# A decoder layer on one core: three activation chunks split straight from PSUM, and x given a second time with its columns on partitions

## The chip, the core and the metric

The kernel runs on one core of a Trainium2 chip. The metric is the device time of one execution in microseconds (us). Five engines matter here, each with its own queue that it works through in order: TensorE (PE in the profile, its weight loads PEld), VectorE (DVE), ScalarE (ACT), GpSimd (POOL) and SyncE (SP). SP issues most of the loads; POOL and ACT issue the others. An engine that waits holds up everything behind it in its own queue.

## The reference, cut to what matters

One layer over 256 rows and 2048 columns, all in float32:

```
h      = rmsnorm(x, g_mix)                       # x * rsqrt(mean(x*x over the row)) * g_mix
proj   = h @ w_in                                # q, k, v of 16 heads, and three gates
o      = stick-breaking / block-sparse / dilated attention, 4 + 6 + 6 heads
merged = sum over the branches of sigmoid(gate) * (o_branch @ w_branch)
x      = x + merged @ w_out
h2     = rmsnorm(x, g_ffn)
gu     = h2 @ w_gu                               # 2 * 5632 columns
x      = x + (silu(gu[:, :5632]) * gu[:, 5632:]) @ w_down
```

q and k of the last 12 heads are normed by row and scaled with `q_gain` and `k_gain`.

## The kernel before

**Products.** A product takes its left factor with the contracted columns on partitions. Each float32 factor is split into a high part, which ScalarE rounds (`copy`, shown as CAST), and a low part, which VectorE subtracts (`tensor_sub`, shown as TENSOR_TENSOR); `split` (lines 104 to 107) issues both. `product` (lines 164 to 169) is then three TensorE instructions: high by high (L167), low weights by high (L168), high weights by low (L169), each 128x128 against 128x512. Weights come in tiles of 128x1024, two steps k of the contraction. The split weights have five rooms each (`w_hi`, `w_lo`), the raw ones four (`w_raw`), and the raw quarters of a pair six (`g_raw`).

**Units.** The first half is a list of units: unit 1 is the v columns of head group 0, unit 2 the first gate, unit 3 the q and k columns of group 0 as a pair. `project` does a single block of columns; `project_pair` does two blocks at once with seven instead of eight products of quarters for the chunks in `WC`, the rest plainly. `begin_pair` already loads and splits the next unit's first quarters. Side work hangs in two lists of generators, `stages` and `slow_stages`; `advance` takes one step of one of them per weight tile. A scheduler orders the instructions of each engine, save where `keep_in_program_order` or `manual_schedule` fixes them.

**The start.** x is loaded in 128x512 pieces (`xc`, `xs`), rows on partitions. TensorE transposes each by four 128x128 instructions against `ident` (`first_columns`, `transpose4`), VectorE multiplies what comes out in PSUM with `g1` (`next_columns`, `to_h`), and the result is split into `h`. `g1` is `g_mix` transposed by TensorE, and `g2` and the q and k gains come the same way from `par`. A few dummy products (`idle`) fill TensorE while the first loads are under way. The rows are squared in unit 1 on ScalarE (`squares`), and their mean gives `rstd`, which `keep_v` multiplies onto the finished v. While the rows are not yet known, v stands in its two PSUM banks (`ps`).

**The gate and up projections.** Eleven units, c = 0 to 10, each a `project_pair` over `w_gu`, then SiLU and product into two tiles `sg`. `to_a` transposes them (four TensorE instructions for each 128 rows, into the PSUM tile `tr`, which has two banks), copies them out (ScalarE, L938), and POOL stores them to `a_mem` in DRAM (L939). The factor of the down projection is read back from there: `take_a` loads a chunk into `a_raw` (POOL, L959) and splits it by L105 into `a_hi` and `a_lo`. For the first three chunks (`ORDER[:EARLY]`, chunks 0, 1 and 2, L968) this is written behind the eleven units, and the scheduler puts it into units 1, 2 and 3 (each carries the chunk of the unit before it) as soon as the data exist; the other eight are taken around the beginning of the down projection.

Of the kernel before, what the change touches and what calls it, by code (L numbers as in the profile page):

```python
# [17 lines left out]
P = 128  # L18
# [33 lines left out]


@with_exitstack
def hybrid_block(ctx: ExitStack, tc: tile.TileContext, x, g_mix, w_in, q_gain, k_gain, w_branch, w_out,
                 g_ffn, w_gu, w_down, rel_bias, onehot, extra, out):
    nc = tc.nc
    x, out = x[0], out[0]

# [10 lines left out]
    nc.scalar.dma_start(gmix, g_mix[0].rearrange("(k p) -> k p", p=P))  # L70

    ident = consts.tile([P, P], F32, name="ident")
    nc.gpsimd.memset(ident, 0.0)
# [26 lines left out]
    def fetch(dst, src):  # L100

        tc.keep_in_program_order(nc.sync.dma_start(dst, src))
# [284 lines left out]
            tc.keep_in_program_order(nc.tensor.matmul(nothing, zeros[:, :P], zeros, start=True, stop=True))  # L387


    NPAR = KT + 2 * H_SOFT  # L390
    par = consts.tile([NPAR, P], F32, name="par")
    tc.keep_in_program_order(nc.gpsimd.dma_start(par[0:KT, :], g_ffn[0].rearrange("(k p) -> k p", p=P)))
    tc.keep_in_program_order(nc.gpsimd.dma_start(par[KT:KT + H_SOFT, :], q_gain[0]))
    tc.keep_in_program_order(nc.gpsimd.dma_start(par[KT + H_SOFT:NPAR, :], k_gain[0]))

    x1 = dram.tile([NT, P, D], F32, name="x1")

    p1 = pool(ph1, "p1", "left")
# [9 lines left out]
    def load_x(c, queue):  # L408
        xc = [half_kb() for _ in range(NT)]
        for t in range(NT):  # L410
            queue(xc[t], x[t * P:(t + 1) * P, c * NB:(c + 1) * NB])
        return xc
# [16 lines left out]
            if pin:  # L429
                tc.keep_in_program_order(sq)  # L430

    ss1 = small.tile([P, NT, 4], F32, name="ss1", bufs=1)
    rstd = small.tile([P, NT], F32, name="rstd", bufs=1)
    g1 = consts.tile([P, KT], F32, name="g1")
    g2 = consts.tile([P, KT], F32, name="g2")
    gq = consts.tile([P, H_SOFT], F32, name="gq")


    V0 = 2 * NH * HD
    xc = [half_kb() for _ in range(NT)]  # L440
    xs = [xc]
# [15 lines left out]
    xs.append(load_x(1, fetch))  # L457
# [5 lines left out]
    xs += [load_x(c, fetch) for c in (2, 3)]  # L463


    columns = {c: [o_raw[:, 4 * i + 2 * t:4 * i + 2 * t + 2, :].rearrange("p h (a q) -> p (h a) q", a=2)
                   for t in range(NT)] for i, c in enumerate(WC)}

    def next_columns(c, t, pt):
        tmp = columns[c][t]  # L470
        nc.vector.tensor_mul(tmp, pt, g1[:, 4 * c:4 * c + 4, None].to_broadcast([P, 4, P]))
        h.put(c, t, tmp)

    held = []

    def first_columns(t, n, w, goes_on=None):

        if not goes_on:
            held.append(tr.tile([P, 4, P], F32, name="tr"))
            for i in range(w):  # L480
                nc.tensor.transpose(held[-1][:, i, :], xc[t][:, (n + i) * P:(n + i + 1) * P], ident)
            if goes_on is not None:
                return
        pt = held[-1]
        k = slice(n, n + w)
        c = columns[0][t][:, k]
        nc.vector.tensor_mul(c, pt[:, 0:w], g1[:, k, None].to_broadcast([P, w, P]))
        nc.scalar.copy(h.hi[:, k, t * P:(t + 1) * P], c)

    def low_part(t):  # L490
# [22 lines left out]
        nc.tensor.matmul(ps0[t], h.plain(t, k)[1], woven(W_HI[k]), start=False, **how)  # L513

    with tc.manual_schedule(engines={mybir.EngineType.PE, mybir.EngineType.DVE, mybir.EngineType.Activation}):
        high(0)
        first_columns(0, 0, 2)
        first_columns(0, 2, 2)
        idle(3)
        high_high(0, 0)  # L520
        first_columns(1, 0, 4, False)
        low(0)
        high(1)
        high_high(0, 1)
        low_part(0)
        high_low(0, 0)
        low_high(0, 0)
        first_columns(1, 0, 4, True)
        low(1)
        low_high(0, 1)  # L530
        high_low(0, 1)
        turned = [transpose4(xs[1][0])]
        high_high(1, 0)
        high_high(1, 1)
        high_low(1, 0)
        high(2)
        low_part(1)
        high_low(1, 1)
        low_high(1, 0)
        low_high(1, 1)  # L540
        low(2)
        high_high(0, 2)
        low_high(0, 2)
        turned.append(transpose4(xs[1][1]))
        high_high(1, 2)
        low_high(1, 2)
        high(3)
        low(3)
        next_columns(1, 0, turned[0])
# [6 lines left out]
        next_columns(1, 1, turned[1])  # L556
        high_low(0, 3)
        high_low(1, 3)


    def rest_of_x():
        for c in range(2, 4):
            for t in range(NT):
                to_h(h, xs[c][t], c, t, g1, c == 3)
                yield
            squares(xs[c - 2], ss1, c - 2, True)
            yield
        squares(xs[2], ss1, 2)
        squares(xs[3], ss1, 3)
# [26 lines left out]
    vec = dram.tile([H_SOFT, NDIST], F32, name="vec")  # L596

    def parameters():
        pp = tr.tile([P, 4 * P], F32, name="tr")
        nc.tensor.transpose(pp[:, :NPAR], par, ident[:NPAR, :NPAR])  # L600
        parT = consts.tile([P, NPAR], F32, name="parT")
        nc.vector.tensor_copy(parT, pp[:, :NPAR])
        nc.vector.tensor_copy(g2, parT[:, 0:KT])
        nc.vector.tensor_mul(gq, parT[:, KT:KT + H_SOFT], parT[:, KT + H_SOFT:NPAR])
# [9 lines left out]
        nc.tensor.matmul(pb[:H_SOFT, :NDIST], rb_sb[:N_BUCKETS, :H_SOFT], oh_sb[:N_BUCKETS, :NDIST], start=True, stop=True)  # L614
# [161 lines left out]
    heads = {}  # L776

    def keep_v(g, ps):
        finish_stages(slow_stages)
# [49 lines left out]
    for (kind, what), after in zip(units, units[1:] + [(None, None)]):  # L829
# [14 lines left out]
                         *((ps0, 4, there) if (kind, what) == ("v", 0) else ()))  # L844
            ahead = begin_pair(*nxt) if nxt else None
        finish_stages(stages)
        if kind == "v":
            keep_v(what, ps)
            if what == 0:
                slow_stages.append(sums_of_h())  # L850
# [80 lines left out]

    a_mem = dram.tile([NF // 4, P, 4, S], F32, name="a_mem")

    def to_a(c, srcs):
        for t in range(NT):
            pt = transpose4(srcs[t])
            st = half_kb().rearrange("p (k q) -> p k q", k=4)
            nc.scalar.copy(st, pt)  # L938
            nc.gpsimd.dma_start(a_mem[c, :, :, t * P:(t + 1) * P], st)  # L939
            yield  # L940
# [175 lines left out]
```

## Time and profile before

| | |
|---|---|
| median of 3 runs | 1387.82 us (1387.64 to 1389.24) |
| the profiled execution's own time | 1387.56 us |
| its span, first to last instruction | 1385.8 us |
| mean granted TensorE clock | 0.994 of full speed |
| PE busy | 1362.3 us, 98% of the span |
| DVE, ACT, POOL busy | 83%, 64%, 8% |

A row of the timeline gives start, duration, engine, line, operation, `out<-in`, shape, count, and in brackets how long the engine was idle before it and what ended that. In a row with a count, the duration is that of the whole group. Neighbouring instructions of an engine overlap by some 0.1 us, so the start of the next is less than start plus duration. A TensorE row shows 0.38 us, while the next starts after 0.215 us. A line in `split` is the same, L105, whichever tile it splits, so one has to go by the names of the tiles.

### The profile page before, as it was taken

To read this page: it belongs to the slowest core of one execution; us is meant where nothing else is said; L and a number is where in the kernel's file an instruction comes from. 1 tells how busy PE (TensorE), PEld (TensorE's weight loads), DVE (VectorE), ACT (ScalarE), POOL (GpSimd) and SP (SyncE) were. 2 spreads that over 40 slices of the span, in tenths; PEclk is the share of its full clock that TensorE was granted. 3 is DMA by queue.
4 is the path that set the end of the run, shared out by engine and by line. 5 is a ranking of instruction groups with operands and counts; after the bars stand their busy time and mean duration, and the time that the engine had idled before them with its cause. 6 is when DMAs were issued, how large, how long until landed. Compare 5 with 4: busy or idle time off the path is not lost.

```text
span 1385.8 us, 17910 instructions
## 1 busy us (share of the span) xinstructions
PE 1362.3 (98%) x6404; PEld 1184.9 (85%) x6404; DVE 1151.7 (83%) x1222; ACT 880.9 (64%) x1140; POOL 109.4 (8%) x173
## 2 busy tenths in 40 slices
PE   9999999999999999999999988999999999999998
PEld 7888888888888888888887877888888888788887
DVE  7888797858989987776698877999999998887785
ACT  7678877767776665445565656667666665564553
POOL 1100000000010112101001001010000010100000
PEclk9999999999999999999999999999999999999999
DMA  8875567576687779877887677678787877767553
GB/s 277 288 255 169 202 181 257 147 242 196 244 286 266 263 228 336 276 220 227 294 276 252 224 244 228 214 259 285 247 277 244 274 216 236 258 239 258 195 178 101
DMA packets 93928, 331.07 MB, mean 239 GB/s; under 512 B 11312, under 2 KB 12928, under 8 KB 93840
## 3 DMA queue, kind: packets, MB, share of 16 engines
q1 hardware_dynamic: 76896, 275.29, 57.1%
q0 software_dynamic: 15760, 53.60, 15.0%
q8 instruction: 50, 0.82, 0.2%
q10 hardware_dynamic: 1184, 1.06, 0.2%
q14 instruction: 38, 0.31, 0.1%
HBM read 292.65 MB, written 16.27 MB: 223 GB/s over the span
## 4 chain that ended last, share of the span: by engine, by line
PE 77%; issue 12%; DMA 4%; ACT 3%; DVE 3%; POOL 1%; POOLq 0%; ACTq 0%; DVEq 0%
PE ps L167 9%; PE ps L168 9%; PE ps L169 9%; PE qs L169 9%; PE qs L168 9%; PE qs L167 9%; PE z L167 4%; PE z L169 4%; PE z L168 4%; DMA a_raw<-a_mem 2%; PE v L167 2%; PE v L168 2%; PE v L169 2%; PE tr L189 1%; ACT w_hi L105 1%
## 5 line engine op out<-in xcount | busy, mean ns | idle before, releaser
L105 DVE TENSOR_TENSOR w_lo<-w_raw,w_hi 128x1024 fp32r<-128x1024 f32 x334 | 405.2, 1221 | 84.7 <-ACT w_hi L105 81.9
L105 ACT CAST w_hi<-w_raw 128x1024 fp32r<-128x1024 f32 x334 | 347.4, 1048 | 177.3 <-PE qs L169 80.1
L105 ACT CAST w_hi<-g_raw 128x1024 fp32r<-128x1024 f32 x184 | 191.5, 1048 | 137.0 <-DVE g_raw L310 45.8
L105 DVE TENSOR_TENSOR w_lo<-g_raw,w_hi 128x1024 fp32r<-128x1024 f32 x184 | 221.3, 1222 | 37.3 <-ACT w_hi L105 34.1
L105 ACT CAST w_hi<-u 128x1024 fp32r<-128x1024 f32 x138 | 143.8, 1047 | 82.9 <-PE qs L169 17.8
L105 DVE TENSOR_TENSOR w_lo<-u,w_hi 128x1024 fp32r<-128x1024 f32 x138 | 167.8, 1221 | 27.4 <-ACT w_hi L105 26.6
L168 PE MATMUL ps<-w_lo,h_hi 128*128 128x512 f32 x360 | 136.7, 380 | 0.0
L169 PE MATMUL ps<-w_hi,h_lo 128*128 128x512 f32 x360 | 136.4, 379 | 0.0
L167 PE MATMUL ps<-w_hi,h_hi 128*128 128x512 f32 x360 | 134.0, 383 | 0.0
L168 PE MATMUL qs<-w_lo,h_hi 128*128 128x512 f32 x332 | 126.4, 381 | 0.0
L169 PE MATMUL qs<-w_hi,h_lo 128*128 128x512 f32 x332 | 125.9, 380 | 0.0
L167 PE MATMUL qs<-w_hi,h_hi 128*128 128x512 f32 x332 | 122.5, 381 | 0.0
L169 PEld LDWEIGHTS ps<-w_hi,h_lo 128*128 128x128 f32 x360 | 68.0, 189 | 9.6
L168 PEld LDWEIGHTS ps<-w_lo,h_hi 128*128 128x128 f32 x360 | 68.1, 189 | 9.3
L167 PEld LDWEIGHTS ps<-w_hi,h_hi 128*128 128x128 f32 x360 | 67.8, 189 | 9.2
L321 DVE TENSOR_TENSOR u<-g_raw 128x1024 f32<-128x1024 f32 x40 | 48.8, 1219 | 26.7 <-DMA g_raw<-in_w_in 18.6
L169 PEld LDWEIGHTS qs<-w_hi,h_lo 128*128 128x128 f32 x332 | 62.8, 189 | 9.4 <-issue 0.6
L168 PEld LDWEIGHTS qs<-w_lo,h_hi 128*128 128x128 f32 x332 | 62.8, 189 | 9.0 <-DVE w_lo L105 0.4
L167 PEld LDWEIGHTS qs<-w_hi,h_hi 128*128 128x128 f32 x332 | 62.7, 189 | 8.6
L167 PE MATMUL v<-w_hi,h_hi 128*128 128x512 f32 x120 | 47.7, 397 | 13.3 <-ACT w_hi L105 13.3
L310 DVE TENSOR_TENSOR u<-u,g_raw 128x1024 f32<-128x1024 f32 x40 | 47.2, 1219 | 0.0
L310 DVE TENSOR_TENSOR g_raw<-g_raw 128x1024 f32<-128x1024 f32 x40 | 47.1, 1218 | 0.0
(398 smaller groups left out, 2950.2 us busy)
## 6 DMA issues: line engine op xcount, KB each, us to landing
w_raw<-in_w_in SPq DMA_DIRECT2D x118, 512.0 KB, 4.7
g_raw<-in_w_gu SPq DMA_DIRECT2D x88, 512.0 KB, 6.1
w_raw<-in_w_gu SPq DMA_DIRECT2D x88, 512.0 KB, 6.6
g_raw<-in_w_in SPq DMA_DIRECT2D x72, 512.0 KB, 6.2
w_raw<-in_w_down SPq DMA_DIRECT2D x64, 512.0 KB, 4.3
u<-g_raw POOLq DMA_DIRECT2D x40, 512.0 KB, 5.5
w_raw<-in_w_branch SPq DMA_DIRECT2D x32, 512.0 KB, 4.8
w_raw<-in_w_out SPq DMA_DIRECT2D x32, 512.0 KB, 4.3
```

The source lines that it names most:

```text
L105: for op in nc.scalar.copy(hi, src), nc.vector.tensor_sub(lo, src, hi.bitcast(F32)):
L167: nc.tensor.matmul(ps, ah, wh, start=start, stop=False, **how)
L168: nc.tensor.matmul(ps, ah, wl, start=False, stop=False, **how)
L169: nc.tensor.matmul(ps, al, wh, start=False, stop=stop, **how)
L189: nc.tensor.transpose(pt[:, i, :], src[:, i * P:(i + 1) * P], ident)
L310: tc.keep_in_program_order(nc.vector.tensor_add(d, d, a))
L321: nc.vector.tensor_add(d, a, b)
```

## The change

Three things:

- **The early chunks of the down projection's factor.** The rooms for chunks 0, 1 and 2 are placed before the eleven units. For these chunks `to_a` splits directly what the transposes left in PSUM (two halves of 128x512), instead of copying, storing, loading and splitting a 128x1024 piece. The stores to `a_mem`, the loads of `a_raw` and their splits are gone for these three.
- **x with columns on partitions.** The host gives x a second time as `across`, already transposed, and the vectors `g_mix`, `g_ffn`, `q_gain`, `k_gain` as one 128x128 array `factors`. The start loads `across` where it loaded `x`, multiplies it in place with `g1`, and splits. The 32 transposes of x, those of `gmix` and `par`, and three small POOL loads are gone. The dummy products become 8 in one go instead of 5 and 3, and the hand-written order of the first products changes.
- **The squares.** The rows of x, still needed for `rstd`, are now loaded in unit 2, in four 128x1024 pieces, into the rooms of the quarters (`g_raw`), and squared there (`row_scale`, a stage of unit 2). `keep_v` of group 0 is the last step of that stage, so v stays in its PSUM banks into unit 2.

TensorE's queue at the start. `tr<-sc` with 128x512 are the dummy products, `tr<-ident` the transposes, `ps` the first unit's products; before:

```order
L387 MATMUL tr<-sc 128x512 x5
L455 MATMUL tr<-ident,gmix 128x16
L481 MATMUL tr<-ident,sc 128x128 x4
L387 MATMUL tr<-sc 128x512 x3
L507 MATMUL ps<-w_hi,h_hi 128x512
L481 MATMUL tr<-ident,sc 128x128 x4
L507 MATMUL ps<-w_hi,h_hi 128x512
L510 MATMUL ps<-w_lo,h_hi 128x512
L513 MATMUL ps<-w_hi,h_lo 128x512 x2
```

The same queue now:

```order
L389 MATMUL tr<-sc 128x512 x8
L492 MATMUL ps<-w_hi,h_hi 128x512
L495 MATMUL ps<-w_lo,h_hi 128x512
L492 MATMUL ps<-w_hi,h_hi 128x512
L495 MATMUL ps<-w_lo,h_hi 128x512
L498 MATMUL ps<-w_hi,h_lo 128x512 x2
```

The transposes are gone, and the dummies stand together.

ScalarE's queue in gate and up unit 1, which carries chunk 0 (`sc<-tr` is the copy of the transposed chunk, `a_hi` the high part of the chunk, `w_hi` those of the weights); before:

```order
L938 COPY sc<-tr 128x512 x2
L105 CAST w_hi<-u 128x1024
L305 COPY sc<-z 128x512
L105 CAST w_hi<-u 128x1024
L105 CAST w_hi<-w_raw 128x1024
L105 CAST w_hi<-g_raw 128x1024
L105 CAST a_hi_10162<-a_raw 128x1024
L105 CAST w_hi<-g_raw 128x1024
```

The same place now:

```order
L107 CAST a_hi_6246<-tr 128x4x128 x2
L107 CAST w_hi<-u 128x1024
L307 COPY sc<-z 128x512
L107 CAST w_hi<-u 128x1024
L107 CAST w_hi<-w_raw 128x1024
L107 CAST w_hi<-g_raw 128x1024 x2
```

The split of the chunk took the place of the copy, and nothing that hangs on a load of the chunk stands between the weights any more. In the same unit VectorE's queue now has

```order
L312 TENSOR_TENSOR u<-u,g_raw 128x1024 x2
L107 TENSOR_TENSOR a_lo_6247<-tr,a_hi_6246 128x4x128 x2
L107 TENSOR_TENSOR w_lo<-u,w_hi 128x1024 x2
L107 TENSOR_TENSOR w_lo<-w_raw,w_hi 128x1024
L312 TENSOR_TENSOR g_raw<-g_raw 128x1024 x2
L107 TENSOR_TENSOR w_lo<-g_raw,w_hi 128x1024 x2
```

where before one `a_lo<-a_raw,a_hi 128x1024` stood between the two `w_lo<-g_raw`. The two half pieces now stand ahead of five weight operations.

ScalarE's queue at the border of unit 2 and unit 3 (`v<-ps,rstd` is `keep_v`, `sc<-qs,rstd` the gate's sigmoid); before:

```order
L105 CAST w_hi<-g_raw 128x1024
L782 ACTIVATE v<-ps,rstd 128x512 x2
L105 CAST w_hi<-g_raw 128x1024 x3
L773 ACT_TABLE_LOAD
L773 ACTIVATE sc<-qs,rstd 128x512 x2
```

Now:

```order
L107 CAST w_hi<-g_raw 128x1024 x3
L771 ACTIVATE v<-ps,rstd 128x512 x2
L761 ACT_TABLE_LOAD
L761 ACTIVATE sc<-qs,rstd 128x512 x2
L107 CAST w_hi<-u 128x1024 x2
```

The scaling of v moved behind all four splits of unit 3's first quarters, next to the sigmoid.

The diff, cut to its core:

```diff
-    consts.tile([P, 72], F32, name="fill")
-    gmix = consts.tile([KT, P], F32, name="gmix")
...
+    consts.tile([P, 276], F32, name="fill")
+    fac = consts.tile([P, P], F32, name="fac")
+    nc.scalar.dma_start(fac, factors)
+    g1, g2 = fac[:, 0:KT], fac[:, KT:2 * KT]
...
-    tc.keep_in_program_order(nc.gpsimd.dma_start(par[0:KT, :], g_ffn[0].rearrange("(k p) -> k p", p=P)))
...
-    fetch(xc[0], x[0:P, 0:NB])
+    fetch(columns[0][0], across[0, 0])
     first_weights(0)
-    fetch(xc[1], x[P:S, 0:NB])
+    fetch(columns[0][1], across[0, 1])
...
-    idle(5)
-    pg = tr.tile([P, 4 * P], F32, name="tr")
-    nc.tensor.transpose(pg[:, :KT], gmix, ident[:KT, :KT])
-    nc.vector.tensor_copy(g1, pg[:, :KT])
+    idle(8)
...
+    def next_columns(c, t):
+        col, g = columns[c][t], g1[:, 4 * c:4 * c + 4]
+        if c == 3:
+            for i in range(4):
+                nc.scalar.activation(col[:, i], col[:, i], AF.Copy, scale=g[:, i:i + 1])
+        else:
+            nc.vector.tensor_mul(col, col, g[:, :, None].to_broadcast([P, 4, P]))
+        h.put(c, t, col)
...
+    def row_scale(ps):
+        halves = [(t, n) for t in range(NT) for n in range(2)]
+        rows = {}
+        for i in range(len(halves) + 2):
+            if i < len(halves):
+                t, n = halves[i]
+                rows[i] = gx.tile([P, 2 * NB], F32, name="g_raw", bufs=6)
+                fetch(rows[i], x[t * P:(t + 1) * P, 2 * n * NB:2 * (n + 1) * NB])
+            if i >= 2:
+                t, n = halves[i - 2]
+                tc.keep_in_program_order(nc.scalar.activation(rows[i - 2], rows[i - 2], AF.Square,
+                                                              accum_out=ss1[:, t, n:n + 1]))
+            yield
...
+        rsqrt_mean(rstd, sst, D, NT)
+        yield
+        keep_v(0, ps)
...
-        if kind == "v":
+        if (kind, what) == ("v", 0):
+            stages.append(row_scale(ps))
+            slow_stages.append(sums_of_h())
...
+    for c in ORDER[:EARLY]:
+        a.place(pe, c)
+
     def to_a(c, srcs):
         for t in range(NT):
             pt = transpose4(srcs[t])
+            if c in ORDER[:EARLY]:
+                a.put(c, t, pt)
+                yield
+                continue
             st = half_kb().rearrange("p (k q) -> p k q", k=4)
             nc.scalar.copy(st, pt)
             nc.gpsimd.dma_start(a_mem[c, :, :, t * P:(t + 1) * P], st)
...
-    for c in ORDER[:EARLY]:
-        take_a(pe, c)
```

More of the change, by code (lines that the diff above doesn't have):

```diff
@@ L54, in hybrid_block @@
 @with_exitstack
-def hybrid_block(ctx: ExitStack, tc: tile.TileContext, x, g_mix, w_in, q_gain, k_gain, w_branch, w_out,
-                 g_ffn, w_gu, w_down, rel_bias, onehot, extra, out):
+def hybrid_block(ctx: ExitStack, tc: tile.TileContext, x, w_in, w_branch, w_out, w_gu, w_down, rel_bias,
+                 onehot, extra, across, factors, out):
     nc = tc.nc
@@ L66, in hybrid_block @@
     dram = ctx.enter_context(tc.tile_pool(name="dram", bufs=1, space=DRAM))
-    consts.tile([P, 72], F32, name="fill")
-    gmix = consts.tile([KT, P], F32, name="gmix")
-    nc.scalar.dma_start(gmix, g_mix[0].rearrange("(k p) -> k p", p=P))
+    consts.tile([P, 276], F32, name="fill")
+    fac = consts.tile([P, P], F32, name="fac")
+    nc.scalar.dma_start(fac, factors)
+    g1, g2 = fac[:, 0:KT], fac[:, KT:2 * KT]
+    q_gain, k_gain = (fac[:, 2 * KT + i * H_SOFT:2 * KT + (i + 1) * H_SOFT] for i in range(2))
     ident = consts.tile([P, P], F32, name="ident")
@@ L430, in squares @@
                 tc.keep_in_program_order(sq)
-    ss1 = small.tile([P, NT, 4], F32, name="ss1", bufs=1)
+    ss1 = small.tile([P, NT, 2], F32, name="ss1", bufs=1)
     rstd = small.tile([P, NT], F32, name="rstd", bufs=1)
-    g1 = consts.tile([P, KT], F32, name="g1")
-    g2 = consts.tile([P, KT], F32, name="g2")
     gq = consts.tile([P, H_SOFT], F32, name="gq")
     V0 = 2 * NH * HD
-    xc = [half_kb() for _ in range(NT)]
-    xs = [xc]
+    columns = {c: [o_raw[:, 4 * i + 2 * t:4 * i + 2 * t + 2, :].rearrange("p h (a q) -> p (h a) q", a=2)
+                   for t in range(NT)] for i, c in enumerate(WC)}
     raws = [wpool.tile([P, 2, NB], F32, name="w_raw", bufs=4) for _ in range(2)]
@@ L447, in hybrid_block @@
     nc.scalar.preload_act_table_set("natural_log_exp_and_others")
-    fetch(xc[0], x[0:P, 0:NB])
+    fetch(columns[0][0], across[0, 0])
     first_weights(0)
-    fetch(xc[1], x[P:S, 0:NB])
+    fetch(columns[0][1], across[0, 1])
     for k in range(1, 4):
         first_weights(k)
-    idle(5)
-    pg = tr.tile([P, 4 * P], F32, name="tr")
-    nc.tensor.transpose(pg[:, :KT], gmix, ident[:KT, :KT])
-    nc.vector.tensor_copy(g1, pg[:, :KT])
-    xs.append(load_x(1, fetch))
+    idle(8)
+    for t in range(NT):
+        fetch(columns[1][t], across[1, t])
     there = []
@@ L462, in hybrid_block, with first_columns @@
         there.append(raw)
[L463 to L484, printed above, removed]
+    for c in range(2, 4):
+        columns[c] = [half_kb().rearrange("p (k q) -> p k q", k=4) for _ in range(NT)]
+        for t in range(NT):
+            fetch(columns[c][t], across[c, t])
+    def next_columns(c, t):
[6 more added lines that the diff above has]
+        h.put(c, t, col)
+    def first_columns(t, n, w):
         k = slice(n, n + w)
         c = columns[0][t][:, k]
-        nc.vector.tensor_mul(c, pt[:, 0:w], g1[:, k, None].to_broadcast([P, w, P]))
+        nc.vector.tensor_mul(c, c, g1[:, k, None].to_broadcast([P, w, P]))
         nc.scalar.copy(h.hi[:, k, t * P:(t + 1) * P], c)
@@ L515, in hybrid_block @@
     with tc.manual_schedule(engines={mybir.EngineType.PE, mybir.EngineType.DVE, mybir.EngineType.Activation}):
+        first_columns(0, 0, 2)
         high(0)
-        first_columns(0, 0, 2)
         first_columns(0, 2, 2)
-        idle(3)
         high_high(0, 0)
-        first_columns(1, 0, 4, False)
         low(0)
+        first_columns(1, 0, 4)
+        high_low(0, 0)
+        low_part(0)
+        high_high(1, 0)
+        high_low(1, 0)
+        low_high(0, 0)
         high(1)
+        low_part(1)
+        low_high(1, 0)
+        low(1)
         high_high(0, 1)
[L525 to L529, printed above, removed]
+        high_high(1, 1)
         low_high(0, 1)
+        low_high(1, 1)
+        high(2)
         high_low(0, 1)
[L532 to L537, printed above, removed]
         high_low(1, 1)
-        low_high(1, 0)
-        low_high(1, 1)
         low(2)
@@ L563, in rest_of_x @@
             for t in range(NT):
-                to_h(h, xs[c][t], c, t, g1, c == 3)
+                next_columns(c, t)
                 yield
-            squares(xs[c - 2], ss1, c - 2, True)
+    def row_scale(ps):
[10 more added lines that the diff above has]
+                                                              accum_out=ss1[:, t, n:n + 1]))
             yield
-        squares(xs[2], ss1, 2)
-        squares(xs[3], ss1, 3)
         sst = small.tile([P, NT], F32, name="sst", bufs=1)
@@ L598, in parameters @@
     def parameters():
[L599 to L604, printed above, removed]
+        nc.vector.tensor_mul(gq, q_gain, k_gain)
         nc.vector.tensor_scalar(gq, gq, SCALE, None, op0=ALU.mult)
@@ L778, in keep_v @@
     def keep_v(g, ps):
-        finish_stages(slow_stages)
+        if g:
+            finish_stages(slow_stages)
         heads["v", g] = v = pa.tile([P, NT, NB], F32, name="v", bufs=1)
@@ L846, in hybrid_block @@
         finish_stages(stages)
-        if kind == "v":
+        if (kind, what) == ("v", 0):
+            stages.append(row_scale(ps))
+            slow_stages.append(sums_of_h())
+        elif kind == "v":
             keep_v(what, ps)
-            if what == 0:
-                slow_stages.append(sums_of_h())
         elif kind == "qk":
@@ L932, in hybrid_block @@
     a_mem = dram.tile([NF // 4, P, 4, S], F32, name="a_mem")
+    WD = (4, 6, 8)
+    ORDER = [0, 1, 2, 4, 3, 6, 5, 8, 7, 9, 10]
+    EARLY = 3
+    a = Chunks(None, "a", NF // 4, WD, False)
+    for c in ORDER[:EARLY]:
+        a.place(pe, c)
     def to_a(c, srcs):
@@ L1084, in hybrid_block @@
     down_pair(2 * NB, elsewhere, in_acc, (nc.scalar, nc.sync))
-_INS = ["x", "g_mix", "w_in", "q_gain", "k_gain", "w_branch", "w_out", "g_ffn", "w_gu", "w_down", "rel_bias"]
+_INS = ["x", "w_in", "w_branch", "w_out", "w_gu", "w_down", "rel_bias"]
 def by_blocks(w):
@@ L1106 @@
     given["onehot"], given["extra"] = distance_tables()
+    given["across"] = np.ascontiguousarray(given["x"][0].reshape(NT, P, 4, 4, P).transpose(2, 0, 4, 3, 1))
+    columns = [np.asarray(inputs[n][0], np.float32) for n in ("g_mix", "g_ffn", "q_gain", "k_gain")]
+    columns = np.concatenate([c.reshape(-1, P) for c in columns]).T
+    given["factors"] = np.zeros((P, P), np.float32)
+    given["factors"][:, :columns.shape[1]] = columns
     arrays, args = {}, []
```

13 lines of the change are left out of this document (2 added, 11 removed).

## The prediction

> **What bounds the kernel now.** First the busy shares: TensorE is busy for 98% of the span, so a change pays only where TensorE waits, runs below full speed, or does work that goes away. Next the waits of TensorE after the start; this row heads them (total us, times, longest), and no other reaches 1 us.
>
> ```profile
> PE v L167 <- ACT w_hi L105: 13.3, 4, 4.2
> ```
>
> The timeline shows where it is. POOL's stores of a finished activation chunk come once in each gate and up unit, so the distance between two is a unit's length (first to fourth, then the last of the undisturbed ones):
>
> ```profile
> 747.60 1.62 POOL L939 DMA_DIRECT2D a_mem<-sc  x2 [32.20 <-ACT sc L938]
> 794.38 1.59 POOL L939 DMA_DIRECT2D a_mem<-sc  x2 [38.51 <-ACT sc L938]
> 840.01 1.60 POOL L939 DMA_DIRECT2D a_mem<-sc  x2 [37.77 <-ACT sc L938]
> 886.78 1.50 POOL L939 DMA_DIRECT2D a_mem<-sc  x2 [38.81 <-ACT sc L938]
> 1125.26 1.54 POOL L939 DMA_DIRECT2D a_mem<-sc  x2 [34.55 <-ACT sc L938]
> ```
>
> The three units that take an early chunk last 46.78, 45.63 and 46.77 us. The six after them last (1125.26 - 886.78) / 6 = 39.75 us each. The excess is 139.18 - 119.25 = 19.93 us. ScalarE, then TensorE, in the first of the three:
>
> ```profile
> 754.40 1.04 ACT L105 CAST w_hi<-g_raw 128x1024 fp32r<-128x1024 f32 x1 [2.69 <-DVE g_raw L310]
> 759.96 1.04 ACT L105 CAST a_hi<-a_raw 128x1024 fp32r<-128x1024 f32 x1 [4.51 <-DMA a_raw<-a_mem]
> 760.91 1.04 ACT L105 CAST w_hi<-g_raw 128x1024 fp32r<-128x1024 f32 x1
> ...
> 758.40 0.38 PE L169 MATMUL z<-w_hi,h_lo 128*128 128x512 f32 x1
> 762.95 0.79 PE L167 MATMUL v<-w_hi,h_hi 128*128 128x512 f32 x1 [4.18 <-ACT w_hi L105]
> 763.54 0.63 PE L167 MATMUL z<-w_hi,h_hi 128*128 128x512 f32 x1
> 763.97 0.63 PE L167 MATMUL ps<-w_hi,h_shi 128*128 128x512 f32 x1
> ...
> 768.48 0.38 PE L169 MATMUL ps<-w_hi,h_slo 128*128 128x512 f32 x1
> ```
>
> The chunk's split stands in ScalarE's queue ahead of two weight splits and waits 4.51 us for its load from `a_mem`. TensorE runs dry for 4.18 us and then works at half pace: a product starts every 0.43 us instead of 0.216. From 758.40 to 768.48 it starts 14 products, which take 14 x 0.216 = 3.02 us at full pace; 10.08 - 3.02 = 7.06 us are lost, as the unit's excess of 7.03 says. A table of stretches shows the clock behind that, for this stall and the two others (columns: stretch, length, PE busy and the count of products that reach into it, granted clock, DMA share, GB/s):
>
> ```profile
> 758.40:768.48 10.08, 5.90 (x16) 0.66 0.55 148
> 805.18:812.80 7.62, 3.38 (x9) 0.78 0.43 84
> 850.80:860.56 9.76, 5.55 (x15) 0.65 0.48 126
> ```
>
> So each stall has two parts, the idle time and a stretch at a lower clock. [...]
>
> **The start.** Here TensorE is busy, but partly with transposes:
>
> ```profile
> 5.38 0.62 ACT L501 CAST w_hi<-w_raw 128x512 fp32r<-128x512 f32 x1 [2.84 <-DMA w_raw<-in_w_in]
> 7.08 0.63 PE L507 MATMUL ps<-w_hi,h_hi 128*128 128x512 f32 x1
> 11.49 1.05 ACT L105 CAST w_hi<-w_raw 128x1024 fp32r<-128x1024 f32 x1 [0.50 <-DMA w_raw<-in_w_in]
> 12.74 1.05 ACT L105 CAST w_hi<-w_raw 128x1024 fp32r<-128x1024 f32 x1 [0.20 <-DMA w_raw<-in_w_in]
> 15.29 0.60 PE L189 MATMUL tr<-ident,sc 128*128 128x128 f32 x4
> 15.65 0.46 PE L167 MATMUL ps<-w_hi,h_hi 128*128 128x512 f32 x1
> 36.73 0.81 PE L614 MATMUL tr<-sc 32*12 32x383 f32 x2
> 37.79 0.38 PE L167 MATMUL qs<-w_hi,h_hi 128*128 128x512 f32 x1
> 54.62 0.38 PE L167 MATMUL ps<-w_hi,h_hi 128*128 128x512 f32 x1
> ```
>
> Unit 3 begins at 54.62. Between 37.79 and 54.62 stand 78 products, 0.2158 us each: the full pace. Units 1 and 2 have 192 products, 41.4 us; from 7.08 to 54.62 they take 47.5.
>
> **The change, part by part.**
>
> *Early chunks: 19.9 us off.* The queues show no operation that waits for a load of the chunk between weights any more, so all three stalls lose their cause. On ScalarE two pieces of 128x512 from `tr` are rounded where they were copied, and the 1.04 us of `a_hi<-a_raw` goes. VectorE gets two pieces for one whole:
>
> ```profile
> L422 DVE TENSOR_TENSOR sc<-tr,g x10: 681/684/692, 16.2 to 709.4; 128x512 f32<-128x512 f32 x10
> L105 DVE TENSOR_TENSOR h_lo<-sc,h_hi x8: 684/685/693, 19.0 to 712.3; 128x512 fp32r<-128x512 f32 x8
> L105 DVE TENSOR_TENSOR a_lo<-a_raw,a_hi x8: 1216/1226/1226, 761.0 to 1206.4; 128x1024 fp32r<-128x1024 f32 x8
> ```
>
> A split's subtraction from PSUM has no row, but a multiplication of that shape from PSUM has, 0.684 us, and the subtraction from SBUF takes 0.685. Two are 1.37 us, against 1.23 before. They come earlier, ahead of the weights of the next sums. Whether TensorE feels it is read from an undisturbed unit, VectorE and then TensorE:
>
> ```profile
> 888.24 1.23 DVE L105 TENSOR_TENSOR w_lo<-u,w_hi 128x1024 fp32r<-128x1024 f32 x1
> 894.35 2.36 DVE L105 TENSOR_TENSOR w_lo<-g_raw,w_hi 128x1024 fp32r<-128x1024 f32 x2
> ...
> 892.73 0.38 PE L168 MATMUL qs<-w_lo,h_shi 128*128 128x512 f32 x1
> 898.35 0.38 PE L168 MATMUL qs<-w_lo,h_shi 128*128 128x512 f32 x1
> ```
>
> The low part of `u` is ready at 889.5 and used at 892.73; that of the first summed quarter at 895.5 and used at 898.35. The margin is 2.8 us, and 1.4 is put on it: no wait. The six stores and three loads on POOL's queue and their traffic go; since nothing but ScalarE's split waited for them, that is worth nothing further.
>
> *x across, factors: 2.1 us off.* I walk the new queues with the old durations. The first columns land as x did (4.45, by the transpose that waited for it). VectorE multiplies, ScalarE rounds and then does the first weights, which land at 5.38; the first product starts at about 6.1 instead of 7.08. The weights for steps 4 and 5 still land at 11.49, behind the same bytes, so their split ends at 12.54; TensorE reaches them at about 14.1 instead of 15.65. From there VectorE sets the pace: a weight tile takes it 1.14 us (1.23, of which neighbours overlap 0.09; a pair takes 2.36 above), a 128x512 piece 0.61 (0.69 less the overlap). It has the low part of steps 6 and 7 ready at 16.7, where TensorE arrives 0.7 us earlier, and of steps 8 and 9 at 21.0, where TensorE arrives at 21.1. From 21.1 on 144 products remain, 31.1 us: unit 3 begins at 52.2 by this walk. ScalarE may hand over later than I count, so I take 52.5, 2.1 us earlier. The most that is possible is full pace from 14.1 on: 168 products and the bias product's 0.8 us (L614), 51.2, a gain of 3.4. The least is nothing: `factors` is 64 KB where `g_mix` was 8, and if it takes the 6.3 us of the slowest group below from an issue at 0.8, it lands at 7.1, 2.6 us late, VectorE's start slips by that and its second of waiting for 12.54 takes up only part. POOL's three small loads had no follower on the path.
>
> *Squares in unit 2: 0.2 us on.* Four loads of 512 KB go through SP's queue among the weights of unit 2. Each moves in 1.25 us (11.49 to 12.74 is one such load), 5 us in all; a weight tile serves 2.59 us of TensorE (12 products), and the loads for unit 2 run several tiles ahead, so they are hidden. On ScalarE eight squares of 128x512 (0.62 us each, below) become four of 128x1024, at 1.05 as its other passes of that size: less work than before, though in another place. What can cost is the scaling of v, which must free `ps` for unit 3:
>
> ```profile
> L428 ACT ACTIVATE sc<-sc x16: 612/618/630, 19.2 to 701.6; 128x512 f32<-128x512 f32 x16
> ...
> 52.27 1.05 ACT L105 CAST w_hi<-g_raw 128x1024 fp32r<-128x1024 f32 x1 [1.54 <-PE qs L169]
> 55.79 1.99 ACT L105 CAST w_hi<-u 128x1024 fp32r<-128x1024 f32 x2
> 62.85 1.05 ACT L105 CAST w_hi<-u 128x1024 fp32r<-128x1024 f32 x1 [2.70 <-DVE u L310]
> ...
> 64.98 0.38 PE L167 MATMUL ps<-w_hi,b_shi 128*128 128x512 f32 x1
> ```
>
> The fourth split of the quarters starts 2.35 us before unit 3 (52.27 against 54.62) and ends at -1.4. The two scalings, 1.27 us together as before, then end at -0.7 and -0.1, so the first bank is free 0.7 us before TensorE needs it; the second is needed only 12 products later. The table load and all that follows on ScalarE come 1.2 us later, relative to unit 3, than before. That carries through VectorE to the split that stood at 62.85 and was used at 64.98: it ends 10.5 us after the border and is needed at 10.36. So 0.1 to 0.3 us are lost; I take 0.2. If the cover were gone altogether, the loss would be 1.2.
>
> *The sum.* 1387.56 - 19.9 - 2.1 + 0.2 = 1365.8 against the profiled execution's own time. The median of the runs stands 0.26 above that execution, so I say 1366.0.
>
> **The rivals.**
>
> *A new wait takes the place of the old one.* The two subtractions stand where VectorE is busiest (sums and weights in one run from 883 to 900). If reading PSUM while TensorE writes it cost more than the 0.684 us row, TensorE would wait in three units. It decides from 2.8 us of lateness on; wholly replaced stalls give 1387.8 - 2, about 1386, half of them 1376. Against it: the multiplications from `tr` ran beside full TensorE work and took as long as the subtractions from SBUF.
>
> [...]
>
> ```profile
> sc<-in_x SPq DMA_DIRECT2D x8, 256.0 KB, 6.3
> ```
>
> [...]
>
> *The change doesn't do what it says.* If the stalls came not from the load but from the 2.69 us wait for VectorE ahead of them, they would stay: 1385.7. Against it: an undisturbed unit shows that same wait, and no stall.
>
> ```profile
> 893.27 2.18 ACT L105 CAST w_hi<-g_raw 128x1024 fp32r<-128x1024 f32 x2 [2.69 <-DVE g_raw L310]
> ```
>
> **How the numbers follow.** The forecast, stalls gone and a gain of 0 to 3.4 at the start, gets 0.80; a new wait in the three units 0.08; a row scale that is late by a little 0.07, by so much that it is slower 0.02; no effect 0.03. The low end is 1387.6 - 19.9 - 3.4 = 1364.3, less 0.3 for the spread of runs. The high end is the forecast without the gain at the start and with the 1.2 us of uncovered ScalarE work, 1387.8 - 19.9 + 1.2 = 1369.1, plus 0.9 into the second rival's field. A difference of 0.2%, 2.8 us, is about what can be told from no change. Faster holds the first case, the little late row scale and nearly all new waits; the no-effect case and the tail of the new waits are the same.
>
> **What would show it.** Right: no `a_hi<-a_raw` row in ScalarE before 1100, the units with early chunks near 40 us, no granted clock below 0.98 in that stage, unit 3 beginning near 52.5. Wrong: a TensorE wait for `w_lo` or `a_lo` in those units; a wait of the first `ps` product of unit 3 for `v`; a first product later than 7.1, held by `fac`; or unit 3 beginning at 54.6 or later.

## The result, and the profile after

The changed kernel takes 1366.53 us (median of 4 runs, 1365.94 to 1367.19) where the kernel before takes 1387.73 us beside it (1386.44 to 1389.24): a ratio of 0.9847, 95% interval 0.983 to 0.9864, or 21.2 us less. The forecast was 1366.0. The profiled execution took 1366.35 us, its span is 1364.6 us, and its mean granted clock is 1.000 where it was 0.994.

The waits of TensorE in the changed kernel (total us, times, longest). The 13.3 us for `v` is gone, and the start's wait for the zeros heads the list:

```profile
PE tr L389 <- DVE sc L401: 1.5, 1, 1.5
PE ps L169 <- ACT w_hi L107: 1.5, 3, 0.5
PE ps L169 <- ACT v L771: 1.0, 1, 1.0
```

The stretches of the units with early chunks (columns as in the prediction's table of stretches): no idle time, no lower clock.

```profile
750.00:790.00 40.00, 40.00 (x191) 1.00 0.73 237
790.00:830.00 40.00, 40.00 (x191) 1.00 0.74 237
830.00:869.00 39.00, 39.00 (x187) 1.00 0.77 250
```

TensorE at the border of units 2 and 3 and once more 10 us later, then ScalarE and VectorE around the border:

```profile
51.84 0.38 PE L171 MATMUL qs<-w_hi,h_lo 128*128 128x512 f32 x1
53.19 0.48 PE L169 MATMUL ps<-w_hi,h_hi 128*128 128x512 f32 x1 [0.97 <-ACT v L771]
63.44 0.38 PE L171 MATMUL qs<-w_hi,h_lo 128*128 128x512 f32 x1
64.36 0.48 PE L169 MATMUL ps<-w_hi,b_shi 128*128 128x512 f32 x1 [0.54 <-ACT w_hi L107]
```

```profile
49.99 1.05 ACT L107 CAST w_hi<-g_raw 128x1024 fp32r<-128x1024 f32 x1 [2.38 <-DMA g_raw<-in_w_in]
51.22 1.06 ACT L107 CAST w_hi<-g_raw 128x1024 fp32r<-128x1024 f32 x1 [0.18 <-DMA g_raw<-in_w_in]
52.45 1.26 ACT L771 ACTIVATE v<-ps,rstd 128x512 f32<-128x512 f32 x2 [0.17 <-DVE rstd L185]
53.73 1.28 ACT L761 ACT_TABLE_LOAD   x1
...
63.26 1.05 ACT L107 CAST w_hi<-u 128x1024 fp32r<-128x1024 f32 x1 [2.70 <-DVE u L312]
52.27 0.15 DVE L185 TENSOR_TENSOR rstd<-rs_y,rs_t 128x2 f32<-128x2 f32 x1
```

Without the wait for v, unit 3 would have begun at 51.84 + 0.22 = 52.06, which is the walk's 52.2. It lost 1.13 us there (1.35 between the two starts, less 0.22) and 0.70 at 63.44, with some 0.5 in single steps around both. What is left of the lead shows at a later mark: POOL's `u<-g_raw` occurs once or twice in each pair unit. Here it is in the second pair unit (before, then after), and at the two ends of the stage with early chunks (712.70 and 889.77 before, then the same two after):

```profile
104.50 0.85 POOL L360 DMA_DIRECT2D u<-g_raw  x1 [36.74 <-DMA w_raw<-in_w_in]
712.70 0.89 POOL L360 DMA_DIRECT2D u<-g_raw  x1 [10.33 <-DVE w_lo L105]
889.77 0.91 POOL L360 DMA_DIRECT2D u<-g_raw  x1 [1.49 <-DMA w_raw<-in_w_gu]
```

```profile
104.45 0.85 POOL L362 DMA_DIRECT2D u<-g_raw  x1 [36.31 <-DMA w_raw<-in_w_in]
711.37 0.89 POOL L362 DMA_DIRECT2D u<-g_raw  x1 [10.94 <-DVE w_lo L107]
868.55 0.91 POOL L362 DMA_DIRECT2D u<-g_raw  x1 [1.56 <-DMA w_raw<-in_w_gu]
```

At 104 the changed kernel is 0.05 us ahead: in these two executions the whole gain of the start has been given back. Between the last two marks it takes 157.18 us where the kernel before took 177.07. So the total came out as forecast while two of its terms did not, and the experiments look for both.

### The profile page after: what moved, and what is told of

It reads as the page before. It is cut to its first block, busy times and chain, and to the rows that moved or that the text cites. A ratio compares the mean times of both kernels' runs of the same rounds, so it can differ in the third digit from the quotient of the medians.

```text
span 1364.6 us, 17794 instructions
## 1 busy us (share of the span) xinstructions
PE 1350.9 (99%) x6370; PEld 1175.0 (86%) x6370; DVE 1148.6 (84%) x1222; ACT 877.6 (64%) x1129; POOL 101.1 (7%) x161
## 4 chain that ended last, share of the span: by engine, by line
PE 86%; DVE 4%; ACT 4%; DMA 3%; issue 2%; SPq 0%; DVEq 0%; POOL 0%; ACTq 0%; POOLq 0%
PE ps L169 10%; PE ps L170 10%; PE ps L171 10%; PE qs L170 10%; PE qs L169 10%; PE qs L171 10%; PE z L170 4%; PE z L171 4%; PE z L169 4%; PE v L170 3%; PE v L169 3%; PE v L171 3%; DVE w_lo L107 2%; ACT w_hi L107 2%; DMA w_raw<-in_w_in 2%
## 5 line engine op out<-in xcount | busy, mean ns | idle before, releaser
L323 DVE TENSOR_TENSOR u<-g_raw 128x1024 f32<-128x1024 f32 x40 | 48.8, 1220 | 25.8 <-DMA g_raw<-in_w_in 17.2
L362 POOL DMA_DIRECT2D u<-g_raw x40 | 35.1, 877 | 232.6 <-DVE w_lo L107 167.2
```

Of the source, the lines that this page charges most:

```text
L323: nc.vector.tensor_add(d, a, b)
L362: nc.gpsimd.dma_start(d, a, accum_op=ALU.add)
```

## The experiments

The times of one group share their runs of the kernel before. Two marks say more than the times where a microsecond matters: `u<-g_raw` near 104 for the start, and the distance of the two `u<-g_raw` near 711 and 869 for the early chunks. In four executions with the start of the kernel before, the first mark lies between 104.45 and 105.03, so half a microsecond there says little.

### Each part alone

`a_only`: the kernel before, with the early chunks alone.

```diff
+    for c in ORDER[:EARLY]:
+        a.place(pe, c)
...
             pt = transpose4(srcs[t])
+            if c in ORDER[:EARLY]:
+                a.put(c, t, pt)
+                yield
+                continue
...
-    for c in ORDER[:EARLY]:
-        take_a(pe, c)
```

> The early chunks alone (split from PSUM), start and squares as before. My theory: the three stalls are the whole of the 19.9 us by unit lengths, so the time is 1387.7 - 19.9 = 1367.8 (1367.0 to 1368.6), the four stores of chunks 0 to 3 stand about 39.75 us apart, unit 3 still begins at 54.6. Rival, the parts depend on each other (the shift at the start changed where the stalls fell): under 17 us of gain, above 1370.

`bc_only`: the changed kernel with that part undone.

> x across, factors and the squares in unit 2, but the early chunks stored, loaded and split as before. My theory: 1387.7 - 1.4 = 1386.3 (1385.5 to 1387.0), since unit 3 began 1.43 us earlier with the whole change and nothing between it and the gate and up units is touched; three waits of about 4.2 us stay. Rival, the start is worth nothing by itself because the stalls or a later load absorb it: 1387.7.

Measured: `a_only` 1366.92 us (1366.50 to 1367.73), ratio 0.9845 (0.983 to 0.986), 21.3 us less than the 1388.18 beside it. `bc_only` 1389.45 us (1388.17 to 1390.70), ratio 1.0009 (0.9999 to 1.0018). Both are outside what was expected, by 0.1 and by 2.4 us. The early chunks are worth the whole gain, and the start and the squares together nothing, at worst 2.5 us of loss. The marks agree: `a_only` passes 104 at 105.03 and `bc_only` at 104.90, and their stages last 157.17 and 178.11 us.

### The split one unit later

`late_split`: the kernel before, with stores, loads and whole splits kept; only the place of the split in the queues changes (a tiny VectorE operation ties it to the next unit).

```diff
+    def late(c):
+        for _ in range(6):
+            yield
+        raw = loaded[c]
+        tc.keep_in_program_order(nc.vector.tensor_scalar(raw[:, 0, 0:2], raw[:, 0, 0:2], 1.0, None, op0=ALU.mult))
+        split(*a.t[c], raw)
+        yield
```

> The kernel before, with the store, the load and the split of the early chunks kept, but each split written one unit after its load. My theory: the stall was only the load's time from issue to landing in front of weight splits in ScalarE's queue, so the waits of 4.2 us go and the time is 1367.8 as without the stores and loads (1367 to 1369.5; the whole split of 1.23 us on VectorE stands at the same place). Rival, the work of the split itself (1.04 us on ScalarE, 1.23 us on VectorE) or the traffic to and from DRAM costs a part: stalls of 1 to 2 us stay in three units and the time is 1371 to 1380.

Measured: 1366.85 us (1366.16 to 1367.17), ratio 0.9843 (0.9828 to 0.9858). The stage takes 157.18 us (711.37 to 868.55), as with the change. The load (POOL's queue) and the split (ScalarE's):

```profile
752.98 0.56 POOL L961 DMA_DIRECT2D a_raw<-a_mem  x1 [2.50 <-PE z L169]
798.22 1.04 ACT L105 CAST a_hi<-a_raw 128x1024 fp32r<-128x1024 f32 x1
```

The split finds its data and waits for nothing. So neither the trip through DRAM nor the work of the split cost TensorE anything; the stalls were the load's latency (4.51 us of waiting on ScalarE in the first of them) in front of two weight splits in a queue that keeps its order, and moving the split does as much as leaving out the trip.

### A second profile of the kernel before

> The kernel before, unchanged, for a second profile. In the first one the quarters of gate and up unit 1 landed late (VectorE waited 6.2 us for g_raw near 691, 4.4 in the kernel with the early chunks alone) and TensorE lost 1.15 us at 717 to 719. If that belongs to the kernel before, it is there again and the units' excess of 19.9 us is not all that the early chunks cost; if it was the chance of one execution, the distance from the last store of gate_mem to the first u<-g_raw after 700 is 182.7 us, as in the others, not 184.1.

Measured: one run, 1390.56 us. TensorE's waits, the stage's two marks, and the first and last stall's stretches:

```profile
PE v L167 <- ACT w_hi L105: 14.6, 4, 4.8
711.80 0.89 POOL L360 DMA_DIRECT2D u<-g_raw  x1 [10.34 <-DVE w_lo L105]
892.32 0.91 POOL L360 DMA_DIRECT2D u<-g_raw  x1 [1.49 <-DMA w_raw<-in_w_gu]
750.00:790.00 40.00, 35.47 (x152) 0.91 0.71 235
...
835.00:892.00 57.00, 52.18 (x236) 0.94 0.64 208
```

The late landing near 691 did not recur: from the last `gate_mem` store (529.13) to 711.80 it is 182.67 us. The stage takes 180.52 us here against 177.07 in the first profile and 178.11 in `bc_only`, so the same three stalls cost 23.3, 19.9 and 20.9 us over 157.18. The three waits themselves add up to 13.9, 12.6 and 13.1 us; the rest, 9.4, 7.3 and 7.8 us, went with the stretches at a lower clock; the mean granted clock is 0.993, 0.994 and 0.993 in these executions and 1.000 in the changed kernel's. The price of a stall changes from one execution to the next, in both parts. The profile on which the forecast rests had the cheapest stalls of the three, and 1.4 us of bad luck elsewhere that made up for it: from 528.64 to 712.70 it took 184.06 us.

### Where the start's gain went

Two theories. R: `rstd` comes last, since its ten small steps stand one by one between VectorE's long ones, from 39.3 to 52.4. L: the quarters of unit 3 land late, because 2 MB of rows stand ahead of them.

`rows_early`: the rows are loaded in unit 1.

```diff
                 next_columns(c, t)
                 yield
+                fetch_row()
```

> The changed kernel with the four loads of rows issued in unit 1 and the squares at the head of unit 2's side work. Theory L: unit 3 began 1.0 us late because the row loads held up the quarters of unit 3 (two waits for g_raw on ScalarE, 2.4 and 0.2 us, ahead of v); then those waits go, unit 3 begins at 52.2 and the time is 1365.5. Theory R: what came last was rstd, whose ten small steps stand one by one between the weights on VectorE over 12 us; then the wait for v at unit 3 stays at 0.5 to 1 us and the time is about 1366.3. Third way: the row loads take the place of weights in unit 1 and TensorE waits there, 1367 or more.

Measured: 1366.28 us (1365.55 to 1368.01), mark at 104.53: nothing gained. TensorE, then ScalarE:

```profile
19.74 0.38 PE L171 MATMUL ps<-w_hi,h_lo 128*128 128x512 f32 x1
21.07 0.70 PE L169 MATMUL ps<-w_hi,h_hi 128*128 128x512 f32 x2 [0.95 <-ACT w_hi L107]
64.43 0.48 PE L169 MATMUL ps<-w_hi,b_shi 128*128 128x512 f32 x1 [0.58 <-ACT w_hi L107]
...
48.47 1.06 ACT L107 CAST w_hi<-g_raw 128x1024 fp32r<-128x1024 f32 x1 [1.80 <-DMA g_raw<-in_w_in]
51.59 1.26 ACT L771 ACTIVATE v<-ps,rstd 128x512 f32<-128x512 f32 x2 [2.07 <-DVE rstd L185]
```

The third way of the expectation happened (1.1 us in unit 1, since the weights now come behind the rows), and theory R holds for the scaling of v, which waits 2.07 us for `rstd`. TensorE no longer waits for v, since it comes to the border 1.1 us later itself, and the second loss stays.

`rstd_short`: the two correcting steps of `rstd` are left out (its values are less exact), so that it is ready at about 41 and the scaling of v stands ahead of all four splits.

```diff
-        rsqrt_mean(rstd, sst, D, NT)
+        rsqrt_mean(rstd, sst, D, NT, 0)
```

> The changed kernel without the two correcting steps of rstd (eight small instructions of VectorE; the values are then less exact). ScalarE's queue then has the scaling of v at about 41, ahead of all four splits of unit 3's quarters; the row loads stay as they are. Theory R (rstd comes last at the border because its steps stand one by one between VectorE's long ones): the wait for v goes (1.13 us lost there in the changed kernel), the sigmoid and the splits of u follow about 1.3 us earlier, so the second loss of unit 3 (1.06 us at 63.4 to 65.2, a wait for w_hi) falls to 0 to 0.5 as well; 1364.4 to 1365.4. Theory L (the quarters land late because of the row loads): the wait for v goes all the same, but TensorE waits for the last quarters or for the splits of u instead and the second loss stays; 1365.4 to 1366.5.

`v_copy`: v is copied out unscaled and multiplied later, so nothing waits for `rstd` at the border; nothing is left out.

```diff
-            stages.append(row_scale(ps))
+            heads["v", 0] = v = pa.tile([P, NT, NB], F32, name="v", bufs=1)
+            for t in range(NT):
+                nc.scalar.copy(v[:, t, :], ps[t])
+            stages.append(row_scale(v))
...
-        keep_v(0, ps)
+        for t in range(NT):
+            nc.vector.tensor_scalar(ps[:, t, :], ps[:, t, :], rstd[:, t:t + 1], None, op0=ALU.mult)
```

> The changed kernel, with v copied unscaled out of its banks by ScalarE in unit 2 (near 36) and multiplied with rstd later by VectorE. Nothing is left out. As for rstd_short: theory R 1364.4 to 1365.4, with unit 3 beginning at about 52.1 and no wait for v; theory L about 1366. The two multiplications of v cost VectorE some 1 us in the stretch 41 to 54, in which it has no idle time, so a wait for w_lo at the head of unit 3 would be the third way, 1366 to 1367.

Measured: 1366.44 us (1364.66 to 1367.67) and 1366.53 us (1365.31 to 1367.42); marks at 104.36 and 104.91. TensorE waits for v in neither, and neither gains; `v_copy` loses 0.6 us near 58 to VectorE, which now also scales v, and 1.0 us near 72 to a `w_hi`. `rstd_short` loses 0.83 us near 40, waiting for the low part of a weight, and 0.74 us near 64. ScalarE and then TensorE in `rstd_short`:

```profile
51.32 1.05 ACT L107 CAST w_hi<-g_raw 128x1024 fp32r<-128x1024 f32 x1 [2.71 <-DMA g_raw<-in_w_in]
52.57 1.05 ACT L107 CAST w_hi<-g_raw 128x1024 fp32r<-128x1024 f32 x1 [0.20 <-PE qs L171]
40.33 0.48 PE L170 MATMUL qs<-w_lo,h_hi 128*128 128x512 f32 x1 [0.56 <-DVE w_lo L107]
64.25 0.48 PE L169 MATMUL ps<-w_hi,b_shi 128*128 128x512 f32 x1 [0.58 <-ACT w_hi L107]
```

Theory R alone has fallen: with `rstd` out of the way the quarters still land at 51.3, and from the end of ScalarE's last work before the table load to the first product with the sums it takes 64.25 - 53.62 = 10.63 us. In the changed kernel it is 64.36 - 53.71 = 10.65. That chain (table load, sigmoid, splits of `u`, VectorE's low parts and sums, the next split) hangs on the landing of the quarters.

`no_rows`: no row loads and tiny squares, so the row scale is not that of x.

> The changed kernel without the four loads of rows and with squares over two columns of 128x2 tiles in place of the rows (the row scale is then not that of x). It gives what the move of the squares costs in all. My theory now: the start gained 2.56 us at the border of units 2 and 3, and unit 3 lost 2.4 of it again through the squares' new place; without them unit 3 begins at 52.1, both waits of unit 3 go, the lead over the kernel before is about 2.5 us still at the first store of a gate, and the time is 1364.1 (1363.5 to 1364.8). Rival: the losses in unit 3 come from the earlier start itself (less time for the loads of the quarters, whose queue is the same): the waits stay, 1365.5 to 1366.5.

Measured: 1366.58 us (1365.43 to 1368.59), mark at 106.78. It tells nothing of the question: the scheduler, with less to do, put other work ahead of the weights on VectorE, and the 48th product starts at 25.6 instead of 19.6 (TensorE waits 1.4 us for a `w_lo` near 17 and then starts a product every 0.43 us until 25). The four executions fall into two pairs: 1367.58, the profiled one, and 1368.59 us at a mean clock of 0.996, and 1365.43 and 1365.57 us at 1.000. The median lies between the pairs and says nothing of 2 us; what the better pair did at the start isn't known.

`eighth_short`: the row loads and `rstd` both made small; seven eighths of the rows and the correcting steps are left out.

```diff
-                rows[i] = gx.tile([P, 2 * NB], F32, name="g_raw", bufs=6)
-                fetch(rows[i], x[t * P:(t + 1) * P, 2 * n * NB:2 * (n + 1) * NB])
+                rows[i] = half_kb()[:, :P]
+                fetch(rows[i], x[t * P:(t + 1) * P, 2 * n * NB:2 * n * NB + P])
```

> The changed kernel with only an eighth of each row loaded and squared (four loads of 64 KB in rooms of their own instead of 512 KB in those of the quarters) and without the correcting steps of rstd; both leave out part of the computation. Theory L (the quarters of unit 3 land at about 50 whatever TensorE does, since 2 MB of rows stand ahead of them; the last split, the table load, the sigmoid and the splits of u follow in a chain of 10.6 us from the end of ScalarE's last work before the table load to the first product with the sums): the quarters land about 4 us earlier, TensorE's room for the split weights sets the chain as before, nothing is lost at 52 and at 63, and the 300th product starts at 75.0 to 76.2 instead of 77.7. Rival: the chain hangs on ScalarE's and VectorE's own order; then the 300th product stays at 77.3 to 77.9. The time itself can tell little of 2 us; by theory L 1364 to 1366.

`rows_early_copy`: `rows_early` and `v_copy` together, nothing left out.

> The changed kernel with the rows loaded in unit 1 and v copied out unscaled and scaled later by VectorE; nothing is left out. By theory L the 1.0 us that unit 1 loses to the row loads stays, v is not waited for, and the chain starts when the last quarter has landed (48.5 to 50): the second loss shrinks from 1.06 to 0 to 0.5. The 300th product starts at 76.8 to 77.4, the time is 1365.5 to 1366.5. Rival as for eighth_short: 77.7 and no gain.

Measured: `eighth_short` 1364.60 us (1364.06 to 1365.14), ratio 0.9826 (0.9812 to 0.9841); the 300th product starts at 75.07. `rows_early_copy` 1366.65 us (1366.39 to 1367.04), ratio 0.9841 (0.9827 to 0.9856), mark at 104.39, the 300th product at 77.61: nothing is lost at 52 and 63, but the 96th product already starts at 33.6 where the changed kernel has it at 30.9 (TensorE waits 1.24 us for a `w_hi` near 20 and then starts a product every 0.43 us from 22.4 to 25.8). In `eighth_short`, ScalarE's last two splits, TensorE at both places, and the mark:

```profile
48.59 1.05 ACT L107 CAST w_hi<-g_raw 128x1024 fp32r<-128x1024 f32 x1 [2.69 <-DMA g_raw<-in_w_in]
50.07 1.06 ACT L107 CAST w_hi<-g_raw 128x1024 fp32r<-128x1024 f32 x1 [0.43 <-DMA g_raw<-in_w_in]
51.22 0.38 PE L169 MATMUL ps<-w_hi,h_hi 128*128 128x512 f32 x1
61.75 0.48 PE L169 MATMUL ps<-w_hi,b_shi 128*128 128x512 f32 x1
101.86 0.85 POOL L362 DMA_DIRECT2D u<-g_raw  x1 [36.31 <-DMA w_raw<-in_w_in]
```

Theory L holds, but not alone: the quarters land earlier (the last two splits start 1.4 and 1.2 us earlier, not the 4 that I expected), no wait is left at the border, the chain still takes 61.75 - 51.13 = 10.62 us, and a lead survives: at 104 it is 104.45 - 101.86 = 2.59 us over the changed kernel. Not all of that belongs to the row loads. This execution began unit 3 at 51.22, 0.84 us before the changed kernel could have (52.06), and 0.63 us of that it had by the 48th product (18.99 against 19.62), before the first row load; the other 1.75 us come from the losses at 52 and 63, which are gone. In the time 1.9 us show (1366.53 - 1364.60, from different groups of runs).

Whether it is the bytes of the rows or the rooms of the quarters, SP's queue tells: the issue of the six quarters, then the time to landing of the three weight loads issued between 25 and 30 (each first in the kernel before, then in the changed one):

```profile
36.01 3.30 SPq L102 DMA_DIRECT2D g_raw<-in_w_in  x6
39.78 2.94 SPq L104 DMA_DIRECT2D g_raw<-in_w_in  x6
DMA to landing us min/median/max: 4.4/5.0/5.1
DMA to landing us min/median/max: 9.9/11.0/11.2
```

In the changed kernel these weights land behind the rows. The first of them was issued at 25.97 and landed at 36.97; ScalarE waited 1.04 us for it, its low part was done at 39.38, and only then, at 39.40, could SP issue the weight load that takes the same room, with the quarters right behind. The last square ended at 39.17, so the rooms of the quarters were free by then and did not hold them up. Issued 3.5 us later, the sixth quarter landed at 51.12 instead of 47.28; in `eighth_short` its split started at 50.07, as soon as it had landed. So it is the bytes, by way of the weights' rooms. And `rstd` counts beside them: in `rows_early` the sixth quarter's split, at 52.75, waited for no load and the chain began behind `rstd`, in `rstd_short` it began behind the quarters, and each keeps the second loss; `eighth_short` is rid of both delays and of the loss. The short load was not tried with the full `rstd`. No version that computes everything can be told from the changed kernel by its time.

### The margin of VectorE in the early units

The rival "a new wait takes the place of the old one" had its price at VectorE. `sub_x3` and `sub_x5` repeat each early subtraction.

```diff
                 a.put(c, t, pt)
+                hi, lo = (z[:, :, t * P:(t + 1) * P] for z in a.t[c])
+                for _ in range(2):
+                    nc.vector.tensor_sub(lo, pt, hi.bitcast(F32))
```

> The changed kernel with each early subtraction done three times (four more pieces of 0.64 us in each of the three units, all ahead of the first summed quarter's low part). My theory: the margin that is left there is 757.94 - 756.16 = 1.8 us (the prediction had 2.8 before and 1.4 put on it), so TensorE waits 2.56 - 1.8 = 0.8 us in each of the three units, 2.3 in all: 1368.8 (1368 to 1370). Rival: VectorE's lateness is taken up elsewhere (the weights' low parts are ready long before they are used): 1366.5.

> As sub_x3 with five subtractions: eight more pieces a unit, six of them ahead of the first low part. By theory TensorE waits 3.84 - 1.8 = 2.0 us for the first and up to 3.3 us in all per unit, 6 to 10 us: 1372.5 to 1376.5, and a lower granted clock only if a single wait comes near the 4.2 us of the old stalls. Rival: 1366.5 to 1368.

Measured: 1369.86 us (1369.50 to 1372.06), ratio 0.9869 (0.9852 to 0.9885), and 1372.56 us (1372.38 to 1373.37), ratio 0.9885 (0.987 to 0.99). TensorE's waits in that stage in `sub_x3`, then the two longest lines in `sub_x5`:

```profile
PE ps L170 <- DVE w_lo L107: 1.6, 2, 0.8
PE qs L170 <- DVE w_lo L107: 0.8, 1, 0.8
...
PE v L169 <- ACT w_hi L107: 2.3, 2, 1.1
PE ps L170 <- DVE w_lo L107: 1.4, 3, 0.8
```

Three waits of 0.8 us, as worked out from the margin of 1.8 us; with the uneven steps between products around each, the stage is 160.58 - 157.18 = 3.4 us longer. Five subtractions make it 6.2 us longer, the low end of what was expected, since two of the eight pieces fall behind the first low part. No wait exceeds 1.1 us and the granted clock stays at 1.00 from 711 to 869. So the margin that the prediction read was real, and the change used about a third of it.

## Why the prediction was right, point by point

- **Early chunks, 19.9 us: mechanism right, size short by 1.4.** The cause is shown by `late_split`, the worth by `a_only`: 21.3 us. The step that was mis-sized is "The excess is 139.18 - 119.25 = 19.93 us": it took one execution's stalls as the kernel's, and they measured 19.9, 23.3 and 20.9 in three (the last in `bc_only`). Both parts of the price differ, the waits from 12.6 to 13.9 us and what went at a lower clock from 7.3 to 9.4; no run shows why.
- **VectorE's margin: right.** 1.8 us were left where 1.4 were expected, and it decides where it was said to.
- **The start, 2.1 us: right up to the border, and worth nothing behind it.** The walk gave 52.2, and TensorE was ready at 52.06; the first product came at 5.68 where 6.1 was walked.
- **Squares in unit 2, 0.2 us: wrong, some 2.4 us.** The step that failed is "the loads for unit 2 run several tiles ahead, so they are hidden". TensorE did not wait for those weights, but they landed up to 11.2 us after their issue, their rooms came free late, and unit 3's quarters, which stand behind them in the same queue, were issued 3.3 to 3.8 us later than before and landed 3.8 to 4.1 us later. And the lateness on ScalarE was counted from unit 3's border, as if the chain behind the quarters moved with the border. In the kernel before it did: the fourth split there waited for TensorE (1.54 us, at 52.27), 5.0 us after the sixth quarter had landed. In the changed kernel the chain starts when the quarters land. The second claim, "The two scalings ... end at -0.7 and -0.1", also failed on `rstd`, which was ready at 52.4.

The DMA engines were not the difference at that place. In the two stretches ahead of the border, with the quarters under way, they moved as much in the changed kernel (DMA share and GB/s are the last two columns) as the 421 and 417 GB/s of the kernel before from 40 to 48:

```profile
44.00:48.00 4.00, 4.00 (x21) 3.49 (x20) 4.00 (x9) 3.35 (x4) 0.00 (x0) 1.00 1.02 414
48.00:52.00 4.00, 4.00 (x20) 3.36 (x18) 4.00 (x7) 1.83 (x2) 0.00 (x0) 1.00 1.03 422
```

The total was right because the two errors cancel: 1387.8 - 21.3 + 0 is 1366.5, as 1387.8 - 19.9 - 1.9 is 1366.0. Of the rivals, the new wait and the missing effect are excluded; the late row scale, which the range calls the second rival, was real, but small: TensorE waited 0.97 us for v and lost 1.13 us there. No run shows the price of a longer wait at that place, for which the range has its last 0.9 us. The wait is also one of the signs of being wrong that the prediction named, the first product of unit 3 waiting for v, and unit 3 began at 53.19, between the forecast's 52.5 and the 54.6 of the kernel before.

## What to carry to other kernels

A load whose consumer stands in an in-order queue ahead of critical work should be consumed a stage later or not be needed at all: here either was worth 21 us, and the later place needed no new data path. A lead won at one place is worth only what the next chain lets through, so ask of each chain behind it whether it moves with TensorE or with a load. And a stall's price taken from a single profile needs a second profile, or a range.

## What was not expected of the hardware

The same instructions at the start reach full pace at different times. In the changed kernel products follow each other every 0.22 us from about 8; in `rstd_short`, whose start is the same, every 0.43 us until 11.1. The granted clock doesn't tell the two paces apart: it is 1.00 from 8 to 11 in the changed kernel, and in the kernel before it is 1.00 from 8.78 to 10.06 as well, where products follow each other every 0.43 us. Of the changed kernel, then of `rstd_short`, two rows of TensorE (two products in each row):

```profile
9.17 0.59 PE L498 MATMUL ps<-w_hi,h_lo 128*128 128x512 f32 x2
9.60 0.59 PE L495 MATMUL ps<-w_lo,h_hi 128*128 128x512 f32 x2
...
8.76 1.06 PE L498 MATMUL ps<-w_hi,h_lo 128*128 128x512 f32 x2
9.61 1.06 PE L492 MATMUL ps<-w_hi,h_hi 128*128 128x512 f32 x2
```

It cost next to nothing there, since VectorE sets the pace soon after: the 48th product starts at 19.62 and 19.75.
